# Feed-forward up projection as seven products of quarter matrices, in a two-layer hybrid backbone step

## The chip, the cores and the metric

The kernel runs on one core of a Trainium2 chip. The metric is the device time of one execution in microseconds; lower is better.

## The reference, cut to what matters

One step of a two-layer backbone on 640 tokens (512 latent, 128 context) of 1,024 channels. Each layer has four parallel attention and pooling branches and then a feed-forward part. The change is in the feed-forward part alone:

```
def conv_ffn(h, w_up, conv_w, w_down):
    u = h @ w_up                         # 640 x 1024 by 1024 x 5504
    ...                                  # uc: width-3 convolution of u along the tokens
    a, gt = jnp.split(uc, 2, -1)
    return (jax.nn.silu(gt) * a) @ w_down
```

The hidden width is 2,752, so u has 5,504 columns: the value half a and the gate half gt.

## The kernel before

All products are exact to about float32: every operand x is split into a high part hi, which is x rounded by ScalarE (L144), and a low part lo = x - hi, made by VectorE (L145). A product is then three TensorE passes: hi*hi, hi*lo, lo*hi. `hT` holds the normed input, channels on partitions, as two such parts.

The hidden width is cut into 21 tiles of 128 and a tile 21 of 64 (for which value and gate share one unit). `up_pair` (L1333) makes a tile: for value and for gate it loads 1,024 x 128 weights (L126, on SyncE's queue, into one of two "raw" buffers), splits them (L144, L145) into one of five "w" buffers, and `tposed` (L531) sums 8 channel blocks x 3 passes into a PSUM bank, for 384 and then for 256 tokens (`CH`): 96 matmuls a tile, of 384 or 256 columns. ScalarE copies the banks to `ub` (L1355, L1357, L1358; four buffers). VectorE convolves: a first tap (L1364) and two taps that add (L1366), for each half. Then ScalarE takes a tanh (L1378), VectorE multiplies twice (L1379, L1381), and the result is split into `gT` (L147 on ScalarE, L148 on VectorE).

`ffn_phase` (L1290) goes through the tiles in groups of 4, 4, 4, 4 and 6 (`GRP`). Tiles 0 and 1 are made together (`up_pair(l, ks[:2])`), since their first matmuls can start before all of hT is there. The down projection of a group (`down`, L1397) is written behind the up projection of the next group; 120 matmuls of 512 columns for four tiles. So on TensorE the order of a layer is: 8 tiles up, down, 4 up, down, 4 up, down, 6 up, down, down. In layer 0 up to two pieces of layer 1's modulation (L370) stand behind each tile, each of which loads 1 MB into a "w" buffer.

The instructions of an engine are in an order that the framework's planner works out when the kernel is built: of the instructions that it takes to be ready, the one written first goes first. An engine then runs them strictly in that order, and waits for semaphores in it.

Of the kernel before, what the change touches and what calls it, by code (L numbers as in the profile page):

```python
# [11 lines left out]
F32 = mybir.dt.float32  # L12
F32R = mybir.dt.float32r
# [17 lines left out]
GRP = (4, 4, 4, 4, 6)  # L31
BLOCKS = ((0, 1), (1, 1), (2, 2), (4, 2), (6, 2))
# [64 lines left out]
class Kernel:  # L97
# [22 lines left out]
    # ---------------------------------------------------------------- weights  # L120
    def load(self, src, a, b):
        raw = self.t(self.rawp, [128, 1024], "raw", bufs=2)
# [34 lines left out]
    # ---------------------------------------------------------------- set up  # L157
    def run(self):
        nc, tc = self.nc, self.tc
        from contextlib import ExitStack  # L160
        with ExitStack() as es:
# [5 lines left out]
            self.rawp = es.enter_context(self.pool("raw", bufs=2))  # L167
# [88 lines left out]
    def modulate_block(self, ks, x):  # L256
        """Channel tiles ks of all token tiles: transpose, modulate and split into hT."""
# [18 lines left out]
    def cond(self):  # L276
        nc = self.nc
        raw = self.t(self.rawp, [128, 1024], "raw", bufs=2)[:16]
# [53 lines left out]
    def small(self, l):  # L332
        """The convolution's taps: loads, and a step later their transposes."""
# [47 lines left out]
    def between(self, gen, mod):  # L381
        """gen's pieces with mod's between them."""
# [5 lines left out]
    def before(self, n, gen, other):  # L388
        """n pieces of gen, all of other, and the rest of gen."""
# [4 lines left out]
    def with_steps(self, gen, steps):  # L394
        """gen's pieces with one of steps after each."""
# [5 lines left out]
    def mod_rows(self, l, b, ps, rows):  # L401
        """Modulation rows 2b and 2b+1 of both streams; gates go to DRAM."""
# [10 lines left out]
    def mod_columns(self, l, b, rows):  # L413
        """Shifts and scales become columns."""
# [18 lines left out]
    def mod_gate(self, l, half):  # L433
        nc, i = self.nc, self.i
        L = self.lay[l]
        w = self.t(self.hp, [128, 2, 1280], "yx", bufs=2)
        g, p = w[:16, 0, :128], w[:16, 1, :256]
# [10 lines left out]
    # ------------------------------------------------------------------ norms  # L448
# [9 lines left out]
    def normed(self, y, xt, junk):  # L458
        """y = xt scaled by its root mean square."""
# [6 lines left out]
    def modulate(self, t, y, f, L, half):  # L466
        """Transpose the normed tile y, modulate it and split it into hT; f (which may be y) is scratch."""
# [19 lines left out]
    def prenorm(self, t, x, L, half):  # L487
        """Norm token tile t and modulate the one before."""
# [10 lines left out]
    def gains(self, l, half, pool, tag, width, bufs):  # L499
        """The gate rows times the norm's gain on all partitions, as [stream][half]."""  # L500
# [10 lines left out]
    # ------------------------------------------------------------- projections  # L511
# [28 lines left out]
    def sweep(self, weights_outer, parts, offs):  # L540
        """Token tiles times weights: parts are (lhs_hi, lhs_lo, w_hi, w_lo) by k. Yields a bank per token tile."""
# [27 lines left out]
    # --------------------------------------------------------------- attention  # L569
    def attention_phase(self, l, mod, banks):  # L570
# [6 lines left out]
        with self.pool("att_r", side="right") as ap:  # L577
# [38 lines left out]
            if l == 0:  # L616
                self.mod_gate(l, 0)
# [4 lines left out]
    def weave(self, chain, fill):  # L622
        """Run the chain; wherever it yields a time, let as much of fill pass as takes the tensor engine that time."""
# [10 lines left out]
    def late_y(self, gen):  # L634
        """A branch's output that takes the place of the one that gen still reads: made where it is first written."""
# [1061 lines left out]
```

## Time and profile before

| | us |
|---|---|
| median of three runs | 2185.1 (2182.97 to 2185.57) |
| span of the profiled execution | 2180.6 |
| TensorE busy in it | 2130.0 (98%) |
| VectorE busy | 1216.8 (56%) |
| ScalarE busy | 855.7 (39%) |
| GpSimd busy | 183.3 (8%) |

The span runs from the first to the last instruction; the device time of a run also holds what lies around it. The time of the profiled execution itself is not listed apart; against the three runs its span is 2.4 to 5.0 us shorter. In the profile PE is TensorE's matmuls, PEld its weight loads, DVE VectorE, ACT ScalarE, POOL GpSimd, SP SyncE; L145 is line 145 of the kernel before.

### The profile page before, as it was taken

The numbers are of one execution on the slowest core, as the hardware profiler recorded it, in microseconds if no ns is written. First come the engines' busy times: TensorE is split into PE (matmuls) and PEld (weight loads), VectorE is DVE, ScalarE is ACT, GpSimd is POOL, SyncE is SP. The second block draws the span as 40 slices with busy tenths as digits, with TensorE's granted clock in tenths as the row PEclk, the third lists the DMA queues.
The fourth block names the chain that finished last, engine by engine and source line by source line (L and its number), as shares of the span: only waits on it lengthen the run. The fifth ranks groups of instructions, "written<-read, shape, count | busy, mean of one in ns | idle before, by whom it ended". The sixth has DMA issues, their size and how long they took to land.

```text
span 2180.6 us, 34629 instructions
## 1 busy us (share of the span) xinstructions
PE 2130.0 (98%) x13815; PEld 1928.2 (88%) x13815; DVE 1216.8 (56%) x2207; ACT 855.7 (39%) x1822; POOL 183.3 (8%) x574
## 2 busy tenths in 40 slices
PE   7999999999999999999999999999999999999998
PEld 4779989998889988989878799999998899999996
DVE  3774454653466636456577744556543665556554
ACT  4554344443353333224255543434433533323322
POOL 1102100001021001000021031000000200000001
PEclk9999999999999999999999999999999999999999
DMA  9513221214544444343332132211124322222222
GB/s 303 202 43 101 56 62 46 59 40 156 186 144 150 152 136 156 116 155 89 120 128 81 38 92 64 59 48 52 38 79 154 117 78 78 78 78 78 78 85 94
DMA packets 230476, 221.74 MB, mean 102 GB/s; under 512 B 16084, under 2 KB 196637, under 8 KB 225195
## 3 DMA queue, kind: packets, MB, share of 16 engines
q1 hardware_dynamic: 214000, 191.91, 28.3%
q10 hardware_dynamic: 12026, 21.55, 2.8%
q0 software_dynamic: 4288, 6.07, 1.1%
q8 instruction: 109, 1.79, 0.3%
q14 instruction: 53, 0.43, 0.1%
HBM read 207.94 MB, written 11.56 MB: 101 GB/s over the span
## 4 chain that ended last, share of the span: by engine, by line
PE 89%; DVE 4%; issue 2%; ACT 2%; DMA 1%; POOL 1%; ACTq 0%; DVEq 0%; POOLq 0%
PE mm L536 17%; PE mm L538 16%; PE mm L537 16%; PE mm L548 5%; PE mm L550 5%; PE mm L549 5%; PE tr L155 4%; PE sc L946 3%; PE py L938 2%; PE mm L1227 2%; PE mm L1229 2%; PE mm L1228 2%; PE py L370 1%; PE sc L548 1%; PE sc L549 1%
## 5 line engine op out<-in xcount | busy, mean ns | idle before, releaser
L536 PE MATMUL mm<-hT,w 128*128 128x384 f32 (+1 forms) x2592 | 821.6, 317 | 1.2 <-ACT slab L859 0.9
L538 PE MATMUL mm<-hT,w 128*128 128x384 f32 (+1 forms) x2592 | 801.6, 309 | 1.5 <-DVE w L145 1.5
L537 PE MATMUL mm<-hT,w 128*128 128x384 f32 (+1 forms) x2592 | 800.7, 309 | 0.0
L536 PEld LDWEIGHTS mm<-hT,w 128*128 128x128 f32 x2592 | 491.0, 189 | 33.4 <-issue 17.1
L538 PEld LDWEIGHTS mm<-hT,w 128*128 128x128 f32 x2592 | 491.0, 189 | 3.1 <-DVE w L145 3.1
L537 PEld LDWEIGHTS mm<-hT,w 128*128 128x128 f32 x2592 | 491.4, 190 | 2.0 <-issue 1.4
L145 DVE TENSOR_TENSOR w<-raw,w 128x1024 fp32r<-128x1024 f32 (+2 forms) x263 | 313.4, 1194 | 133.0 <-ACT w L144 131.5
L144 ACT CAST w<-raw 128x1024 fp32r<-128x1024 f32 (+2 forms) x263 | 269.3, 1027 | 205.0 <-PE mm L550 37.3
L1364 DVE TENSOR_SCALAR cv<-ub,taps 128x641 f32<-128x641 f32 x86 | 47.7, 555 | 203.3 <-ACT ub L1358 192.9
L1366 DVE SCALAR_TENSOR_TENSOR cv<-ub,taps,cv 128x641 f32<-128x641 f32 x172 | 152.2, 885 | 5.4
L548 PE MATMUL mm<-w,gT 128*128 128x512 f32 (+1 forms) x352 | 141.4, 402 | 0.0
L549 PE MATMUL mm<-w,gT 128*128 128x512 f32 (+1 forms) x352 | 138.9, 394 | 0.0
L550 PE MATMUL mm<-w,gT 128*128 128x512 f32 (+1 forms) x352 | 138.8, 394 | 0.0
L1209 ACT ACTIVATE th<-mm,cols 128x384 f32<-128x384 f32 (+1 forms) x128 | 67.4, 527 | 148.2 <-PE mm L538 147.9
L1355 ACT COPY ub<-mm 128x384 f32<-128x384 f32 x86 | 41.4, 481 | 164.5 <-PE mm L538 164.4
L1236 DVE SCALAR_TENSOR_TENSOR th<-th,mm 128x384 f32<-128x384 f32 x96 | 45.8, 483 | 100.6 <-PE mm L1229 92.7
L548 PEld LDWEIGHTS mm<-w,gT 128*128 128x128 f32 (+1 forms) x352 | 66.2, 188 | 23.8 <-issue 7.4
L1357 ACT COPY ub<-mm 128x128 f32<-128x128 f32 x86 | 23.0, 267 | 162.4 <-PE mm L538 162.3
L1227 PE MATMUL mm<-yx,w 128*128 128x384 f32 (+1 forms) x256 | 82.8, 323 | 0.0
L1429 DVE TENSOR_TENSOR acc<-acc,mm 128x512 f32<-128x512 f32 x64 | 44.0, 687 | 65.3 <-PE mm L550 64.7
L155 PE MATMUL tr<-cst,P 128*128 128x128 f32 x462 | 67.1, 275 | 13.2 <-DVE P L914 9.2
L550 PEld LDWEIGHTS mm<-w,gT 128*128 128x128 f32 (+1 forms) x352 | 66.0, 188 | 15.7
(305 smaller groups left out, 3152.1 us busy)
## 6 DMA issues: line engine op xcount, KB each, us to landing
w<-in_w_mod_dram SPq DMA_DIRECT2D x46, 1024.0 KB, 4.8
raw<-in_ffn_w_up_dram SPq DMA_DIRECT2D x84, 512.0 KB, 3.9
raw<-in_w_gate_dram SPq DMA_DIRECT2D x64, 512.0 KB, 4.0
raw<-in_ffn_w_down_dram SPq DMA_DIRECT2D x40, 512.0 KB, 3.7
raw<-in_w_in_dram SPq DMA_DIRECT2D x23, 512.0 KB, 4.1
raw<-in_w_out_dram SPq DMA_DIRECT2D x16, 512.0 KB, 6.7
x<-x ACTq DMA_DIRECT2D x14, 512.0 KB, 4.8
raw<-in_w_branch_dram SPq DMA_DIRECT2D x12, 512.0 KB, 3.2
```

The source lines that it names most:

```text
L144: nc.scalar.copy(hi, src)
L145: nc.vector.tensor_tensor(out=lo, in0=src, in1=hi.bitcast(F32), op=ALU.subtract)
L155: self.nc.tensor.transpose(out, in_, ident)
L536: nc.tensor.matmul(ps, lhsT=hi[:, k, :], rhs=self.hT[:, 0, k, o:o + n], start=k == 0, stop=False)
L537: nc.tensor.matmul(ps, lhsT=hi[:, k, :], rhs=self.hT[:, 1, k, o:o + n], start=False, stop=False)
L538: nc.tensor.matmul(ps, lhsT=lo[:, k, :], rhs=self.hT[:, 0, k, o:o + n], start=False, stop=k == KT - 1)
L548: nc.tensor.matmul(ps, lhsT=lh[:, c], rhs=hi, start=q == 0, stop=False)
L549: nc.tensor.matmul(ps, lhsT=lh[:, c], rhs=lo, start=False, stop=False)
L550: nc.tensor.matmul(ps, lhsT=ll[:, c], rhs=hi, start=False, stop=q == n - 1)
L1209: self.anchor = nc.scalar.activation(th[:, :n], pg[:, :n], AF.Tanh, scale=0.5, bias=L['bh'][:, 8 * br + m:8 * br + m + 1]).ins
L1227: nc.tensor.matmul(pb[:, :n], lhsT=hi[:, 0, ms], rhs=y[:, 0, a, cs], start=a == 0, stop=False)
L1366: nc.vector.scalar_tensor_tensor(out=cv, in0=ub[:, j:j + 641], scalar=tp[:, j:j + 1], in1=cv, op0=ALU.mult, op1=ALU.add)
```

## The change

Tiles 1 to 20 of each layer (40 in all) go through a new `up_strassen` in place of `up_pair`; tile 21 moves to the front and is made together with tile 0 by `up_pair` as before (`TILES`). The tile's product, 640 tokens x 1,024 channels by 1,024 channels x 256 columns, is cut into quarters: tokens in two halves of 320, channels in two halves of 512, columns in value and gate. Seven products of quarters (Winograd's form of Strassen's algorithm) replace eight: 7 x 4 channel blocks x 3 passes = 84 matmuls of 320 columns. Sums of token quarters are made once a layer (`combine_tokens`, GpSimd and VectorE, then split), in room of the "yx" tiles, a new "S" tile and hT's own quarter (1,0). Differences of weight quarters are made for each tile: four subtractions of 128 x 512 on GpSimd in the raw buffers, and 3.5 splits of 1,024 columns in four "w" buffers where there were two splits in two. The outputs come from three banks, one of which goes on accumulating after it has been read.

The convolution's first tap goes from VectorE to ScalarE, and the product with the value half from VectorE to GpSimd, for all tiles. There are four raw buffers in place of two; the last residual tile takes a raw buffer, the scratch for GpSimd's DMA descriptors is 4,096 bytes, and `mod_gate` takes the "rows" tile in the feed-forward part in place of a "yx" tile. Lines that only drop comments are left out below.

```
+TILES = (21,) + tuple(range(21))
+HALF_TOK = TOK // 2
+RAWS = 4
+DMA_SCRATCH = 4096
...
@@ ffn_phase
-            ks = list(range(f0, f0 + n))
+            ks = list(TILES[f0:f0 + n])
...
                 gt += self.up_pair(l, ks[:2])
+                self.combine_tokens()
...
-                gt += self.up_pair(l, [k])
+                gt += self.up_strassen(l, k)
...
-                    self.mod_gate(l, 1)
+                    self.mod_gate(l, 1, hold())
...
+    def combine_tokens(self):
+        nc, hT = self.nc, self.hT
+        H = HALF_TOK
+        quarter = lambda i, j: hT[:, :, 4 * j:4 * j + 4, H * i:H * i + H]
...
+        S4 = quarter(1, 0)
...
+        for c in (slice(0, 192), slice(192, H)):
+            for i, j in ((0, 0), (1, 0), (1, 1), (0, 1)):
+                q = quarter(i, j)
+                nc.gpsimd.tensor_tensor(out=f[i, j][:, :, c], in0=q[:, 0, :, c].bitcast(F32),
+                                        in1=q[:, 1, :, c].bitcast(F32), op=ALU.add)
+            a11, a21, a22, a12 = [f[x][:, :, c] for x in ((0, 0), (1, 0), (1, 1), (0, 1))]
+            v = nc.vector
+            v.tensor_tensor(out=a22, in0=a21, in1=a22, op=ALU.add)
+            v.tensor_tensor(out=a21, in0=a11, in1=a21, op=ALU.subtract)
+            v.tensor_tensor(out=a11, in0=a22, in1=a11, op=ALU.subtract)
+            v.tensor_tensor(out=a12, in0=a12, in1=a11, op=ALU.subtract)
+            for S, x in ((S2, a11), (S1, a22), (S3, a21), (S4, a12)):
+                self.split(S[:, 0, :, c], S[:, 1, :, c], x)
+        self.A = {1: quarter(0, 0), 2: quarter(0, 1), 3: S4, 4: quarter(1, 1), 5: S1, 6: S2, 7: S3}
+
+    def up_strassen(self, l, k):
...
+        b11, b21, b12, b22 = ra[:, :512], ra[:, 512:], rg[:, :512], rg[:, 512:]
+        tile = lambda: self.t(self.wp, [128, 2, 1024], "w", F32R)
+        W1 = tile()
+        self.split(W1[:, 0], W1[:, 1], ra)
+        W4 = tile()
+        self.split(W4[:, 0, :512], W4[:, 1, :512], b22)
+        sub = lambda out, x, y: nc.gpsimd.tensor_tensor(out=out, in0=x, in1=y, op=ALU.subtract)
+        sub(b11, b12, b11)
+        sub(b12, b22, b12)
+        sub(b22, b22, b11)
+        W2 = tile()
+        self.split(W2[:, 0], W2[:, 1], rg)
+        sub(b21, b21, b22)
+        W3 = tile()
+        self.split(W3[:, 0], W3[:, 1], ra)
+        B = {1: (W1, 0), 2: (W1, 512), 3: (W4, 0), 4: (W3, 512), 5: (W3, 0), 6: (W2, 512), 7: (W2, 0)}
...
+        Q = self.ps("sc")[:, :H]
+        P = self.ps("mm")[:, :H]
+        product(Q, 1, True)
+        copy(first(ub[0]), Q)
+        product(P, 2, True)
+        add(first(ub[0]), P)
+        product(Q, 6, False)
+        copy(first(ub[1]), Q)
+        R = self.ps("mm")[:, :H]
+        product(R, 5, True)
+        copy(second(ub[1]), R)
+        product(Q, 7, False)
+        add(second(ub[1]), Q)
+        product(R, 3, False)
+        add(first(ub[1]), R)
+        product(Q, 4, False)
+        copy(second(ub[0]), Q)
+        return self.gated(l, [(k, 0, ub[0]), (k, 1, ub[1])])
...
@@ gated (the second half of up_pair before)
-            nc.vector.tensor_scalar(cv, ub[:, 0:641], tp[:, 0:1], None, op0=ALU.mult)
+            nc.scalar.activation(cv, ub[:, 0:641], AF.Copy, scale=tp[:, 0:1])
...
-            nc.vector.tensor_tensor(out=th[:np_], in0=th[:np_], in1=a[:np_], op=ALU.mult)
+            nc.gpsimd.tensor_tensor(out=th[:np_], in0=th[:np_], in1=a[:np_], op=ALU.mult)
```

Here copy is a ScalarE copy from the bank and add a VectorE addition of the bank to what stands in `ub`; "first" is the first 320 tokens, "second" the others, in two pieces of 192 and 128.

## Rows read from the trace of the kernel before

**Rows 1.** The page: the span, and busy time, share and instructions of TensorE.
```profile
span 2180.6 us, 34629 instructions
PE 2130.0 (98%) x13815; PEld 1928.2 (88%) x13815; DVE 1216.8 (56%) x2207; ACT 855.7 (39%) x1822; POOL 183.3 (8%) x574
```

**Rows 2.** Busy time by stretch, layer 1: PE, PEld, DVE, ACT, POOL, clock, DMA.
```profile
1711.60:1715.00 3.40, 3.40 (x15) 3.40 (x14) 3.19 (x7) 3.00 (x7) 0.54 (x1) 0.50 0.57 160
...
1720.76:1826.87 106.11, 106.11 (x733) 106.11 (x732) 68.28 (x86) 40.35 (x80) 3.65 (x42) 1.00 0.27 80
1826.87:1854.71 27.84, 27.84 (x122) 22.56 (x121) 9.56 (x12) 11.08 (x17) 0.55 (x6) 1.00 0.27 76
1854.71:1911.00 56.29, 56.29 (x385) 56.28 (x384) 31.92 (x38) 19.22 (x37) 1.67 (x18) 1.00 0.24 75
2023.02:2100.42 77.40, 77.40 (x529) 77.39 (x528) 47.61 (x57) 26.35 (x51) 2.06 (x21) 1.00 0.30 91
```

**Rows 3.** Timeline of TensorE: start, us, instruction (a matmul's end is modelled).
```profile
418.97 1.05 PE L946 MATMUL sc<-slab,stg 96*128 96x320 f32 x6
...
806.14 1.90 PE L370 MATMUL py<-w,silu_c 128*2 128x512 f32 x16
...
899.85 0.33 PE L536 MATMUL mm<-hT,w 128*128 128x384 f32 x1
...
906.61 0.28 PE L536 MATMUL mm<-hT,w 128*128 128x256 f32 x1
...
912.23 0.29 PE L538 MATMUL mm<-hT,w 128*128 128x256 f32 x1
```

**Rows 4.** Groups by form: busy us, mean ns of one, idle before and releasers.
```profile
L145 DVE TENSOR_TENSOR w<-raw,w 128x1024 fp32r<-128x1024 f32 x245 | 299.8, 1225 | 120.7 <-ACT w L144 119.4
L145 DVE TENSOR_TENSOR hT<-yx,hT 128x512 fp32r<-128x512 f32 x30 | 19.8, 686 | 1.0 <-ACT hT L144 0.6
L1366 DVE SCALAR_TENSOR_TENSOR cv<-ub,taps,cv 128x641 f32<-128x641 f32 x172 | 152.2, 885 | 5.4
L148 DVE SCALAR_TENSOR_TENSOR gT<-tf,gT 128x641 fp32r<-128x641 f32 x42 | 34.7, 826 | 29.3 <-ACT gT L147 29.3
L1429 DVE TENSOR_TENSOR acc<-acc,mm 128x512 f32<-128x512 f32 x64 | 44.0, 687 | 65.3 <-PE mm L550 64.7
L1355 ACT COPY ub<-mm 128x384 f32<-128x384 f32 x86 | 41.4, 481 | 164.5 <-PE mm L538 164.4
L1002 POOL TENSOR_TENSOR T<-T,cst 128x896 f32<-128x896 f32 x8 | 16.9, 2112 | 24.5 <-DMA T<-zd 18.4 <-DVE m L1575 6.1
L536 PEld LDWEIGHTS mm<-hT,w 128*128 128x128 f32 x2592 | 491.0, 189 | 33.4 <-issue 17.1 <-ACT w L144 6.9 <-ACT ub L1358 3.5
```

**Rows 5.** Timeline of VectorE and GpSimd where both are at work.
```profile
636.64 2.35 DVE L145 TENSOR_TENSOR w<-raw,w 128x1024 fp32r<-128x1024 f32 x2
637.46 1.58 POOL L453 TENSOR_SCALAR ms<-ss 128x1 f32<-128x1 f32 x1 [4.09 <-ACT yx L462]
...
1343.60 2.11 POOL L1002 TENSOR_TENSOR T<-T,cst 128x896 f32<-128x896 f32 x1 [3.13 <-DMA T<-zd]
1344.48 2.31 DVE L145 TENSOR_TENSOR w<-raw,w 128x1024 fp32r<-128x1024 f32 x1
...
1017.62 0.59 POOL L445 TENSOR_TENSOR yx<-yx 16x128 f32<-16x128 f32 x1
1017.93 0.97 DVE L1366 SCALAR_TENSOR_TENSOR cv<-ub,taps,cv 128x641 f32<-128x641 f32 x1
...
1740.77 1.68 DVE L1366 SCALAR_TENSOR_TENSOR cv<-ub,taps,cv 128x641 f32<-128x641 f32 x2
1741.79 0.10 POOL L1346 MEMSET ub<- 128x1 f32 x1 [3.34 <-DVE cv L1366]
```

**Rows 6.** Timeline: token tile 3's last split, both layers; layer 0's first down matmul.
```profile
648.05 0.68 DVE L145 TENSOR_TENSOR hT<-yx,hT 128x512 fp32r<-128x512 f32 x1
...
764.07 0.47 PE L548 MATMUL mm<-w,gT 128*128 128x512 f32 x1
...
1718.56 0.69 DVE L145 TENSOR_TENSOR hT<-yx,hT 128x512 fp32r<-128x512 f32 x1
```

More of the change, by code (lines that the diff above doesn't have):

```diff
@@ L431, in mod_columns, with mod_gate @@
                 nc.vector.tensor_tensor(out=o, in0=o, in1=col(L['gpre'][half]), op=ALU.mult)
[L433 removed]
+    def mod_gate(self, l, half, w):
         nc, i = self.nc, self.i
         L = self.lay[l]
[L436 to L437 removed]
+        g, p = w[:16, :128], w[:16, 128:384]
         nc.gpsimd.dma_start(out=g, in_=L['mod'][half].rearrange("s k p -> (s k) p"))
@@ L1327, in ffn_phase @@
             for half in range(2):
-                self.mod_gate(nxt, half)
+                self.mod_gate(nxt, half, hold())
         self.down(l, *pend)
@@ new lines, in up_strassen, with product, copy, add @@
+    def up_strassen(self, l, k):
+        nc, i = self.nc, self.i
+        w = i['ffn_w_up'][l].rearrange("(k p) n -> p k n", p=128)
+        ra, rg = [self.load(w[:, :, s * D_FF + 128 * k:s * D_FF + 128 * k + 128], KT, 128)[0] for s in range(2)]
+        b11, b21, b12, b22 = ra[:, :512], ra[:, 512:], rg[:, :512], rg[:, 512:]
[14 more added lines that the diff above has]
+        B = {1: (W1, 0), 2: (W1, 512), 3: (W4, 0), 4: (W3, 512), 5: (W3, 0), 6: (W2, 512), 7: (W2, 0)}
+        H = HALF_TOK
+        def product(ps, m, start):
+            W, o = B[m]
+            A = self.A[m]
+            for q in range(4):
+                hi, lo = W[:, 0, o + 128 * q:o + 128 * q + 128], W[:, 1, o + 128 * q:o + 128 * q + 128]
+                nc.tensor.matmul(ps, lhsT=hi, rhs=A[:, 0, q, :], start=start and q == 0, stop=False,
+                                 skip_group_check=True)
+                nc.tensor.matmul(ps, lhsT=hi, rhs=A[:, 1, q, :], start=False, stop=False, skip_group_check=True)
+                nc.tensor.matmul(ps, lhsT=lo, rhs=A[:, 0, q, :], start=False, stop=q == 3, skip_group_check=True)
+        ub = [self.t(self.fp, [128, 643], "ub", bufs=4) for _ in range(2)]
+        for u in ub:
+            nc.gpsimd.memset(u[:, 0:1], 0.0)
+            nc.gpsimd.memset(u[:, 513:514], 0.0)
+            nc.gpsimd.memset(u[:, 642:643], 0.0)
+        first = lambda u: [(u[:, 1:1 + H], slice(0, H))]
+        second = lambda u: [(u[:, 1 + H:513], slice(0, 512 - H)), (u[:, 514:642], slice(512 - H, H))]
+        def copy(places, ps):
+            for u, c in places:
+                nc.scalar.copy(u, ps[:, c])
+        def add(places, ps):
+            for u, c in places:
+                nc.vector.tensor_tensor(out=u, in0=u, in1=ps[:, c], op=ALU.add)
+        Q = self.ps("sc")[:, :H]
[16 more added lines that the diff above has]
+        return self.gated(l, [(k, 0, ub[0]), (k, 1, ub[1])])
@@ L1368, in up_pair @@
             conv[k, s] = cv
-        for k in ks:
+        for k in dict.fromkeys(k for k, _, _ in work):
             gt = self.t(self.gp, [128, 2, 642], "gT", F32R, bufs=8)
@@ L1395, in unit_pair, with down @@
         return v[:, 0], v[:, 1]
-    def down(self, l, g, f0, gts):
+    def down(self, l, g, gts):
         nc, i = self.nc, self.i
@@ L1413, in down @@
                 rows = i['ffn_w_down'][l]
-                if n1 == 128:
+                if n1 == 128 and pr[-1][0] == k + 1:
                     u = self.unit(rows[128 * k:128 * k + 256, hs].rearrange("(a p) n -> p a n", p=128), 2, 512)
                 else:
-                    u = self.unit_ragged(rows, k, hs)
+                    u = self.unit_ragged(rows, [x[0] for x in pr], hs)
                 for b, (kk, gt, np_) in enumerate(pr):
@@ L1450, in residual @@
         if t == 2:
-            x = self.t(self.fp, [128, D], "x", bufs=1)
+            x = self.t(self.rawp, [128, 1024], "raw", bufs=RAWS)
         else:
```

37 lines of the change are left out of this document (23 added, 14 removed).

## The prediction

> **What bounds the kernel now.** I read the page first, for who is busy: TensorE works through 98% of the span [rows 1]. Then the stretches of layer 1's feed-forward part, where TensorE has no gap at all, neither in four up tiles (56.3 us) nor in the down products of four tiles (27.8 us), while VectorE is busy for 31.9 of 56.3 us and GpSimd for 1.7 [rows 2]. So a matmul saved there is time saved, as long as the other engines keep up. Then TensorE's timeline, for the price of a matmul: from 899.85 to 906.61 stand 39 of 384 columns, 173 ns each; from 906.61 to 912.23 47 of 256 columns, 120 ns each; six of 320 columns, in another stage, take 1.05 us, of which the last one's modelled end is 0.31, so about 148 ns each [rows 3]. Last I looked for places where VectorE and GpSimd work at once, since the change gives GpSimd work [rows 5].
>
> **TensorE.** A tile is now 48 x 0.173 + 48 x 0.120 = 14.1 us; four of them are the 56.3 us of rows 2. After, 84 matmuls of 320 columns at 0.147 (the mean of the two prices) are 12.3 us. 40 tiles x 1.76 = **-70.4 us**. Tile 21 only moves. In layer 0 two pieces of modulation behind a tile add 1.9 us [rows 3], before as after.
>
> **VectorE and GpSimd.** What they do to each other: at 1344.48 VectorE starts a split of 1,024 columns beside a GpSimd addition that ends at 1345.71. The split takes 2.31 us, where the mean is 1.225; it ends 1.08 us after GpSimd [rows 4, 5]. At 1017.93 a convolution tap stretches to 0.97 us and ends 0.69 us after GpSimd's L445, where the mean is 0.885. The other way round, a GpSimd operation on 128 x 1 waits through two splits for 1.58 us (637.46). So a VectorE operation with two inputs in SBUF and a GpSimd operation that reads SBUF do not run together; they share something exclusive. A memset of GpSimd passes beside a tap in 0.10 us, and operations that read PSUM are not counted among those that share.
>
> Work of this shared kind for one new tile, by whole durations [rows 4]:
> - weight splits on VectorE: 3 x 1.225 + 0.686 = 4.36; four subtractions of 512 on GpSimd, at 2.112 us / 896 = 2.36 ns an element, 4 x 1.21 = 4.83. Together 9.2.
> - gating: four taps x 0.885, the product behind the tanh and the split of gT, both as L148, 0.83 each: 5.2 on VectorE; the product of 641 on GpSimd 1.5. Together 6.7.
>
> That is 15.9 us a tile against TensorE's 12.3. It is the upper end. If only the stretches that really excluded each other count (1.08 and 0.69 of VectorE's durations, GpSimd whole), it is 7.9 + 6.3 = 14.3. Two splits in a row take 2.35 and two taps 1.68 [rows 5], so a follower costs 1.13 and 0.80: with these, 8.7 + 6.3 = **15.0**, which I take. VectorE's additions from banks (shorter than the 0.69 us of a 512-column one) read PSUM and fit beside GpSimd.
>
> A stage of down products has 27.8 us of TensorE and little VectorE work, so a backlog can be worked off there; what matters is each run of up tiles: 6 new tiles, 4, 4, 6 in each layer. The weights of a run's first tile come ready during the stage before; tile 1 leaves 12.3 - 9.2 = 3.1 us of the shared time free, and the last weights of a tile are not needed before its fourth product, 3 x 1.76 = 5.3 us in. So a run has 8.4 us of grace; from its third tile on it falls behind by 15.0 - 12.3 = 2.7 us a tile in layer 1, and by 0.7 behind modulation in layer 0.
> - Runs of four: 2 x 2.7 is less than 8.4, no stall: 49.3 instead of 56.3, four times, -28.
> - Last run, layer 1: 4 x 2.7 - 8.4 = 2.4 late, 73.9 + 2.4 instead of 77.4 [rows 2]: -1.1. Layer 0, where modulation covers two tiles: -3.5.
> - **First runs.** They have no grace, because the sums of token quarters come in there. GpSimd adds 4 x 768 and 4 x 512 elements, 12.1 us; VectorE has 8 operations of 768 and 8 of 512 columns, 13.1 us, all of the shared kind: 25.2. They cannot start before token tile 3 is split (1719.25 and 648.73, rows 6). From there on the shared work is 1.4 (last splits of hT) + 25.2 + 11.6 (gating of tiles 21 and 0) + 6 x 9.2 + 4 x 6.7 (the gating of the last two tiles can wait for the down stage) - 1.9 (splits made earlier) = 118.2, at 15.0 / 15.9 of it 111.5; four products, 7.0 us, follow the last weights. Layer 1 ends its run at 1719.25 + 118.5 = 1837.8, before at 1826.9 [rows 2]: +10.9. Layer 0 ends at 767.2, before at 764.07 [rows 6]: +3.2. Without the shared work both would be 17.6 us earlier than before.
>
> Sum: -28 - 1.1 - 3.5 + 10.9 + 3.2 = -18.5. So about 52 of the 70.4 us are given back as waits for weights. At 15.9 the same steps give +17.6, +9.9, -28, +2.5, -1.5: +0.5. At 14.3 they give +5.7, -2.0, -28, -3.5, -3.5: -31.3.
>
> **The rest.** Banks: a bank that goes on accumulating must be read within one product, 1.76 us; a copy takes under 0.48 us [rows 4], but may stand behind a weight split's cast on ScalarE. Now such a wait is 3.5 us in the whole kernel [rows 4]. I take +2, with 0 and +40 (1 us a tile) as ends. ScalarE, 19.2 us in 56.3 now [rows 2], gets one and a half casts and two taps more a tile and stays under TensorE. `mod_gate` puts GpSimd's subtractions behind its DMA waits, three times in layer 0; I take 0, at most a few us, since layer 0 has the modulation as cover. Weight DMAs keep number and size, at 0.24 to 0.30 of the engines [rows 2]: 0. More raw buffers elsewhere and the smaller descriptor scratch: 0, some 5 us either way. A long stall can halve TensorE's clock for a while, as in the 3.4 us from 1711.6 (0.50, rows 2), behind a stretch in which it mostly waited for hT: at most some 2 us each.
>
> Total -16.5. The profiled span is 4.5 us under the median, and I leave what lies around it as it is: 2185.1 - 16.5 = **2169**.
>
> **Rivals.**
> 1. *The two engines hardly hold each other up.* VectorE alone has about 11 us a tile, under 12.3; then only the token sums show, some 5 us a layer: -70.4 + 10 + 2, **2127**. For it: one tap alone shows the hold, by 0.08 us, and the memset passes. Against it: 2.31 and 0.97 end where a full exclusion puts them [rows 5]. The note under "VectorE Performance Modes" of the Trainium skill's page "Advanced Engine Details and Errata" names only VectorE's two-port modes as blocking GpSimd, which gives this case; the trace disagrees with it on the split of two tensors.
> 2. *No change.* Every operation excludes the other engine for all of its duration, 15.9 a tile: +0.5 + 2, **2188**. Against it: 1.08 and 0.69 are less than the whole durations. The Trainium skill's page "SBUF — State Buffer", "SBUF: two separate sides", says that the shared ports are an exclusive lock held for the whole instruction, for VectorE operations with two SBUF inputs against GpSimd operations that read; the trace agrees on who excludes whom, less on the length.
> 3. *Slower: GpSimd is starved and the weights come late everywhere.* The subtractions feed two of the four weight splits. A GpSimd operation waits while VectorE runs one operation behind another (1.58 us, of which 1.4 waiting), and ScalarE, which rounds the difference next, stands in its order with bank copies queued behind it, which TensorE needs. With 1.5 us of this a tile in which neither engine gets on, 17.4 a tile: first runs +28.7 and +21.0, runs of four -24.4 together, last runs +8.5 and +4.5, banks +2: +40, **2225**. It decides from about 15.8 us a tile on. For it: the order of each engine is fixed ahead, and the planner may not know of the exclusion. Against it: VectorE often waits for ScalarE (29.3 us before the gT splits alone, rows 4), and there GpSimd gets its turn.
>
> **How the numbers follow.** My forecast (14.3 to just under 15.8 a tile) 0.50, rival 1 0.15, rival 2 0.13, rival 3 0.22. About 4.4 us, 0.2%, is what a measurement of this kernel can tell from no change. Faster: 0.50 + 0.15 = 0.65. Same: 0.13. Slower: 0.22. The forecast's own range is 2150 to 2182. The range for 8 in 10 takes in rival 2, most of rival 1 and the nearer part of rival 3: 2130 to 2208.
>
> **What would show it.** The 84 matmuls should stand 0.147 us apart. In the runs of four TensorE should be almost without gaps, about 49 us; in the first run of each layer its idle time should be some 20 to 28 us, released by the weight splits of VectorE or ScalarE, and VectorE's splits and taps should show stretched durations (over 2 us and near 1.5 us) beside GpSimd's. If these durations stay at 1.22 and 0.89, rival 1 holds. If the runs of four stall too, with weight loads waiting in every tile, rival 3 does. I am wrong if banks, not weights, release TensorE, or if the time goes to another stage.

## The result and the profile after

| | us |
|---|---|
| before, median of four runs on the same chip | 2185.3 (2183.0 to 2187.7) |
| after, median of four runs | 2303.3 (2303.1 to 2305.5) |
| ratio | 1.0544, 95% interval 1.0529 to 1.0559 |

The change costs 118 us; predicted were 16 less. First the page of the changed kernel, against [rows 1]:

```profile
span 2301.3 us, 34235 instructions
PE 2121.1 (92%) x13335; PEld 1886.6 (82%) x13335; DVE 1377.7 (60%) x2349; ACT 987.4 (43%) x2004; POOL 527.7 (23%) x794
```

480 matmuls are gone (40 tiles x 12), but TensorE is busy for only 9 us less, since for some of the time it runs at half speed; and its idle time has gone from 51 to 180 us. GpSimd has gone from 183 to 528 us. Where the time went, by stretches of TensorE's timeline in layer 1 (from a first to a last matmul):

| us | before | predicted | after |
|---|---|---|---|
| the pair's first matmul to the first down matmul | 118.3 | 129.2 | 155.3 |
| first run of four | 56.3 | 49.3 | 59.5 |
| second run of four | 56.3 | 49.3 | 59.4 |
| last run | 77.4 | 76.3 | 92.0 |

Layer 0 loses as much: its first down matmul stands at 793.0 instead of 764.1 (predicted 767.2), its runs of four take 74.3 and 63.4 instead of 64.3 and 61.8, its last run 102.2 instead of 81.0; the prediction's steps give 57.3, 54.8 and 77.5 for the three. (The last run has six whole tiles now and had five and a half, the first half a tile more; the prediction counted it so.)

Busy time by stretch in layer 1, which answers to [rows 2] (PE, PEld, DVE, ACT, POOL, granted clock, DMA share, GB/s); the first run's Strassen tiles, a run of four, the last run, and one tile of the last run, from one wait to the next:

```profile
1797.36:1924.52 127.16, 83.94 (x507) 81.22 (x506) 93.90 (x105) 54.93 (x96) 64.61 (x71) 0.83 0.19 53
1954.54:2014.00 59.46, 53.22 (x338) 52.40 (x338) 41.85 (x51) 29.70 (x51) 24.10 (x33) 0.94 0.28 81
2129.95:2221.93 91.98, 78.89 (x506) 76.74 (x505) 66.95 (x79) 44.14 (x77) 40.90 (x49) 0.96 0.28 81
2175.37:2192.11 16.74, 12.85 (x86) 12.32 (x85) 12.20 (x15) 7.78 (x15) 8.55 (x11) 1.00 0.23 63
```

Read the last line first. A tile takes 16.74 us, TensorE is busy for 12.85 of them; VectorE's 12.20 and GpSimd's 8.55 add up to 20.75, more than the tile. Laid on one time axis, one of the two or both are at work for 15.74 of 16.74 us, for 5.0 of them both by the record. VectorE's additions from banks take no longer beside GpSimd (0.48 us for 320 columns with it and without); in most of the other overlaps one is held by the other. The groups by form show it in the durations, against [rows 4]; the last two lines have shortest, median and longest of the taps and of three of four differences, in ns:

```profile
L149 DVE TENSOR_TENSOR w<-raw,w 128x1024 fp32r<-128x1024 f32 x285 | 356.3, 1256 | 172.2 <-ACT w L148 167.4 <-PE mm L1397 0.9
L1472 DVE SCALAR_TENSOR_TENSOR cv<-ub,taps,cv 128x641 f32<-128x641 f32 x172 | 196.5, 1199 | 3.9 <-ACT cv L1470 3.6
L1377 POOL TENSOR_TENSOR raw<-raw,raw 128x512 f32<-128x512 f32 x120 | 182.0, 1517 | 310.5 <-DVE w L149 298.5 <-DMA raw<-in_ffn_w_up_dram 6.7 <-ACT ub L1409 1.2
L1487 POOL TENSOR_TENSOR tf<-tf,cv 128x641 f32<-128x641 f32 x42 | 74.1, 1764 | 85.0 <-DVE tf L1485 85.0
L1353 POOL TENSOR_TENSOR gT<-hT 128x768 f32<-128x768 f32 x8 | 16.4, 2079 | 0.0
...
L1472 DVE SCALAR_TENSOR_TENSOR cv<-ub,taps,cv x172: 871/882/1940, 662.0 to 2227.0; 128x641 f32<-128x641 f32 x172
L1377 POOL TENSOR_TENSOR raw<-raw,raw x120: 1263/1306/1876, 645.7 to 2203.6; 128x512 f32<-128x512 f32 x120
```

In the mean a tap takes 1.20 us instead of 0.885, a difference on GpSimd 1.52 where 1.21 was worked out.

The timeline shows the two places where TensorE stands. The first six lines are layer 1's token sums, the rest is one wait of the last run (start, us, instruction, in brackets the idle time before it and what released it):

```profile
1786.21 0.69 DVE L149 TENSOR_TENSOR hT<-yx,hT 128x512 fp32r<-128x512 f32 x1 [0.20 <-ACT hT L148]
...
1811.64 1.53 POOL L1487 TENSOR_TENSOR tf<-tf,cv 128x641 f32<-128x641 f32 x1
1813.13 15.45 POOL L1353 TENSOR_TENSOR gT<-hT 128x768 f32<-128x768 f32 x8
...
1819.10 2.54 DVE L1357 TENSOR_TENSOR gT<-gT,gT 128x768 f32<-128x768 f32 x1 [3.45 <-POOL gT L1353]
1821.68 1.90 DVE L1358 TENSOR_TENSOR gT<-gT,gT 128x768 f32<-128x768 f32 x1
...
1833.30 0.64 PE L1394 MATMUL mm<-yx,w 128*128 128x320 f32 x1 [30.09 <-ACT yx L148]
...
2168.32 3.13 POOL L1377 TENSOR_TENSOR raw<-raw,raw 128x512 f32<-128x512 f32 x2 [0.87 <-DVE w L149]
2171.41 1.58 POOL L1487 TENSOR_TENSOR tf<-tf,cv 128x641 f32<-128x641 f32 x1
2178.71 1.88 POOL L1377 TENSOR_TENSOR raw<-raw,raw 128x512 f32<-128x512 f32 x1 [5.72 <-DVE w L149]
...
2173.80 0.83 DVE L152 SCALAR_TENSOR_TENSOR gT<-tf,gT 128x641 fp32r<-128x641 f32 x1 [4.43 <-ACT gT L151]
...
2178.55 5.36 DVE L1472 SCALAR_TENSOR_TENSOR cv<-ub,taps,cv 128x641 f32<-128x641 f32 x4
...
2173.02 0.74 ACT L151 ACTIVATE gT<-tf 128x641 fp32r<-128x641 f32 x1 [4.70 <-POOL tf L1487]
2173.67 1.99 ACT L148 CAST w<-raw 128x1024 fp32r<-128x1024 f32 x2
2175.57 0.46 ACT L1409 COPY ub<-sc 128x192 f32<-128x192 f32 x2
2175.93 1.05 ACT L148 CAST w<-raw 128x1024 fp32r<-128x1024 f32 x1
2176.88 1.55 ACT L1470 ACTIVATE cv<-ub,taps 128x641 f32<-128x641 f32 x2
2178.33 0.41 ACT L1409 COPY ub<-sc 128x320 f32<-128x320 f32 x1
...
2178.79 0.41 PE L1394 MATMUL sc<-yx,w 128*128 128x320 f32 x1 [3.12 <-ACT ub L1409]
```

The sums: hT's last split in this stretch ends at 1786.9, the first sum starts at 1813.13, behind a gate product; TensorE, which had done three products that need no sums (36 matmuls), stood for 30.1 us. In the last run: GpSimd's gate product ends at 2173.0, only then ScalarE rounds gT, and behind that, in its fixed order, come casts, copies and taps, and at 2178.33 the copy of the bank that TensorE wants for its third product. In layer 1 there is such a wait, of 1.5 to 3.1 us, in nearly every tile from the third of a run on.

The clock has a part too. Its mean is 0.970 (before 0.998): mostly behind waits TensorE is granted 0.5 (1.2 of 2.4 GHz) for a while, in 21 stretches of 139.5 us in all. One of 34.1 us is for the most part its idle time at layer 1's sums. In the others a matmul of 320 columns starts 0.267 us after the one before instead of 0.147. 316 matmuls start in these stretches; at 0.12 us more for 320 columns, and others in proportion, some 41 us is my estimate of what the clock costs. In the run of four above, with two stretches of 3.4 us at 0.50, TensorE is busy for 53.2 us, and 49.3 of them would do at the full clock.

### The profile page after: what moved, and what is told of

It reads as the page before. It is cut to its first block, busy times and chain, and to the rows that moved or that the text cites. A ratio compares the mean times of both kernels' runs of the same rounds, so it can differ in the third digit from the quotient of the medians.

```text
span 2301.3 us, 34235 instructions
## 1 busy us (share of the span) xinstructions
PE 2121.1 (92%) x13335; PEld 1886.6 (82%) x13335; DVE 1377.7 (60%) x2349; ACT 987.4 (43%) x2004; POOL 527.7 (23%) x794
## 5 line engine op out<-in xcount | busy, mean ns | idle before, releaser
L149 DVE TENSOR_TENSOR w<-raw,w 128x1024 fp32r<-128x1024 f32 (+2 forms) x343 | 410.9, 1204 | 182.0 <-ACT w L148 176.5
L148 ACT CAST w<-raw 128x1024 fp32r<-128x1024 f32 (+2 forms) x343 | 333.7, 979 | 264.0 <-PE sc L553 71.3
L539 PE MATMUL mm<-hT,w 128*128 128x256 f32 (+1 forms) x1312 | 425.1, 324 | 0.6 <-ACT hT L148 0.4
L541 PE MATMUL mm<-hT,w 128*128 128x256 f32 (+1 forms) x1312 | 406.5, 310 | 1.5 <-DVE w L149 1.5
L540 PE MATMUL mm<-hT,w 128*128 128x256 f32 (+1 forms) x1312 | 405.6, 309 | 0.0
L539 PEld LDWEIGHTS mm<-hT,w 128*128 128x128 f32 x1312 | 248.2, 189 | 22.2 <-issue 17.1
L1377 POOL TENSOR_TENSOR raw<-raw,raw 128x512 f32<-128x512 f32 x120 | 182.0, 1517 | 310.5 <-DVE w L149 298.5
L541 PEld LDWEIGHTS mm<-hT,w 128*128 128x128 f32 x1312 | 248.2, 189 | 3.1 <-DVE w L149 3.1
L540 PEld LDWEIGHTS mm<-hT,w 128*128 128x128 f32 x1312 | 248.6, 189 | 1.8 <-issue 1.4
L1472 DVE SCALAR_TENSOR_TENSOR cv<-ub,taps,cv 128x641 f32<-128x641 f32 x172 | 196.5, 1199 | 3.9 <-ACT cv L1470 3.6
L1394 PE MATMUL sc<-yx,w 128*128 128x320 f32 x160 | 60.5, 378 | 55.8 <-ACT ub L1409 55.8
L1394 PE MATMUL sc<-hT,w 128*128 128x320 f32 x320 | 102.6, 321 | 9.3 <-DVE ub L1413 7.0
L1394 PE MATMUL mm<-hT,w 128*128 128x320 f32 x320 | 100.9, 315 | 4.5 <-ACT ub L1409 4.4
L1397 PE MATMUL sc<-hT,w 128*128 128x320 f32 x320 | 100.1, 313 | 1.0 <-DVE w L149 0.8
L1487 POOL TENSOR_TENSOR tf<-tf,cv 128x641 f32<-128x641 f32 (+1 forms) x44 | 79.5, 1807 | 91.1 <-DVE tf L1485 91.1
L1396 PE MATMUL sc<-hT,w 128*128 128x320 f32 x320 | 100.3, 313 | 0.0
L1397 PE MATMUL mm<-hT,w 128*128 128x320 f32 x320 | 99.5, 311 | 0.0
```

The source lines that it names most:

```text
L148: nc.scalar.copy(hi, src)
L149: nc.vector.tensor_tensor(out=lo, in0=src, in1=hi.bitcast(F32), op=ALU.subtract)
L539: nc.tensor.matmul(ps, lhsT=hi[:, k, :], rhs=self.hT[:, 0, k, o:o + n], start=k == 0, stop=False)
L540: nc.tensor.matmul(ps, lhsT=hi[:, k, :], rhs=self.hT[:, 1, k, o:o + n], start=False, stop=False)
L541: nc.tensor.matmul(ps, lhsT=lo[:, k, :], rhs=self.hT[:, 0, k, o:o + n], start=False, stop=k == KT - 1)
L1377: sub = lambda out, x, y: nc.gpsimd.tensor_tensor(out=out, in0=x, in1=y, op=ALU.subtract)
```

## The experiments

Theory **T**: VectorE and GpSimd exclude each other, and the sum of their work paces a Strassen tile. Theory **S**: the token sums come late by GpSimd's order. Rivals: **G**, ScalarE's in-order queue, held behind a late GpSimd product; **B**, the banks that must be read in time; **E**, the other edits; **D**, the chain from difference to weights, not the load; **W**, the amount of work in the first run, whatever its order. Times of a single run stand beside 2183 to 2185 us of the kernel before on the same chip.

**The other edits alone.**
```
-                self.combine_tokens()
-                gt += self.up_strassen(l, k)
+                gt += self.up_pair(l, [k])
```


> All tiles go through the ordinary product of 96 matmuls; the token sums and weight differences are not needed and not made. The other edits stay: first tap on ScalarE, gate product on GpSimd, four raw buffers, tile 21 first. Theory T (in a Strassen tile VectorE and GpSimd, which exclude each other, are busy one or the other for 15.7 of 16.7 us, and that sets the pace): an ordinary tile has only some 9 us of such work against 14.1 us of TensorE, so no new waits: 2178 to 2195 us, as before. Rival E (the moved tap and gate product themselves cost, by copies of banks standing behind them on ScalarE): over 2220, with waits of TensorE for the copies in most tiles.


2184.7 us: E falls. Its rows are what ordinary tiles take in this order of tiles (first run with the rest of the pair, a run of four, a last run of six):
```profile
1722.56:1821.25 98.69, 98.69 (x683) 98.69 (x682) 53.80 (x64) 48.49 (x93) 14.70 (x46) 1.00 0.25 71
1851.16:1907.71 56.55, 56.55 (x386) 56.55 (x386) 25.75 (x28) 24.02 (x44) 5.64 (x21) 1.00 0.24 75
2019.57:2104.17 84.60, 84.60 (x578) 84.60 (x577) 40.54 (x44) 35.85 (x66) 9.11 (x29) 1.00 0.28 82
```

**No weight differences.**
```
-        sub(b11, b12, b11)
...
-        sub(b21, b21, b22)
```


> Left out: the four weight differences of GpSimd in each Strassen tile (the weights go into the same splits undiffered, so the output is not the reference's). Everything else stays, all matmuls too. Theory T: the shared time of VectorE and GpSimd falls from 15.7 to some 10 us a tile, under TensorE's 12.3; runs of four in layer 1 go from 59.4 to 49.3-51 us, the last run from 92 to 74-77; the first run keeps its wait of some 30 us for the token sums. In all 2185 to 2220. Rival B (the banks that go on accumulating must be read in time by a ScalarE that works in order, whatever the load): runs of four stay above 57, time above 2270.


2201.6 us; runs of four 51.5, last run 78.2, the wait at the sums still there (27 us). With four GpSimd operations fewer per tile, same matmuls, same banks and same copies, three quarters of what the later runs had over TensorE's own time (49.3 and 74.0) is gone: B falls.

**Differences and gate product on VectorE.**
```
-        sub = lambda out, x, y: nc.gpsimd.tensor_tensor(out=out, in0=x, in1=y, op=ALU.subtract)
+        sub = lambda out, x, y: nc.vector.tensor_tensor(out=out, in0=x, in1=y, op=ALU.subtract)
...
-            nc.gpsimd.tensor_tensor(out=th[:np_], in0=th[:np_], in1=a[:np_], op=ALU.mult)
+            nc.vector.tensor_tensor(out=th[:np_], in0=th[:np_], in1=a[:np_], op=ALU.mult)
```


> The four weight differences and the gate product go from GpSimd to VectorE (a difference of 512 columns should take 0.69 us there instead of 1.54, the product 0.83 instead of 1.76). Theory T: the union of both engines falls from 15.7 to about 14.6 us a tile, VectorE nearly alone: still over 12.3, so waits stay but are smaller: runs of four 53 to 57, last run of layer 1 some 83, in all 2250 to 2280. Rival G (the loss is GpSimd's place in the fixed order, gT's rounding standing on ScalarE behind a late GpSimd product): waits vanish with GpSimd, runs of four 49 to 51, in all 2190 to 2225. Rival B: no change, 2295 to 2310.


2220.5 us, 83 less than after, by giving the busier engine more to do. The total lies in G's range, the runs of four (52.9) lie between the two. But the two tiles from 2097.05 to 2125.32 (second row) show what paces them:
```profile
2056.62:2139.95 83.33, 79.07 (x506) 76.75 (x505) 74.13 (x104) 45.20 (x77) 1.26 (x24) 0.96 0.30 89
2097.05:2125.32 28.27, 26.55 (x172) 24.96 (x171) 27.50 (x39) 16.59 (x30) 0.63 (x12) 1.00 0.27 75
```
VectorE is busy for 27.50 of 28.27 us, 13.8 a tile, and the waits of this run are for weights (the longest 1.0 and 2.0 us, released by ScalarE's and VectorE's halves of a split). T has the mechanism, and its figure was too high: VectorE needs 13.8 us a tile, not 14.6. Part of the 83 us is won at the sums, where TensorE waits 18.4 us instead of 30.1, with no gate product ahead of them on GpSimd.

**A late gate product.** The gate product and the split of gT were to be issued behind the next tile's second copy.
```
+        last = copy(first(ub[1]), Q)
+        with self.tc.issue_after(last):
+            self.finish()
```


> Same instructions, other order: the gate product on GpSimd and the split of gT of a tile are issued behind the next tile's copy of the bank that stalls now, so that this copy can no longer stand on ScalarE behind the rounding of gT. Theory T: the shared work per tile is the same, so the pace stays 16 to 17 us a tile, the waits only change their place or releaser; 2290 to 2315. Rival G: the wait of 3.4 us a tile at the third product goes, with the halved clock behind it: runs of four 50 to 53, in all 2225 to 2260.


2300.1 us, which tells nothing: in the runs of layer 1 ScalarE's order came out as it was, since gT already stood behind that copy. So the next was made.

**A later split of gT,** two tiles on, behind the very copy that TensorE waits for:
```
+        last = copy(first(ub[0]), Q)
+        with self.tc.issue_after(last):
+            self.finish(2)
```


> The same instructions, but ScalarE's rounding of gT of a Strassen tile is issued behind the copy of the bank of the first product two tiles later, which is the copy that TensorE waits for now; so that copy can no longer stand behind a rounding that waits for GpSimd. Theory T (VectorE and GpSimd together are busy 15.7 of 16.7 us a tile): at best the 0.8 us go in which both wait for ScalarE; runs of four 57 to 60 us, in all 2285 to 2306, with new releasers of the waits. Rival G (ScalarE's in-order queue behind GpSimd is what costs): the 3.4 us per tile and the halved clock behind them go: runs of four 50 to 53, in all 2225 to 2260.


2282.9 us; runs of four 54.7 and 56.1, last run 86.0. G has a part: 20 us. What remains fits T; a tile of the last run:
```profile
2161.45:2177.01 15.56, 12.88 (x84) 12.32 (x84) 12.22 (x15) 7.88 (x16) 8.45 (x12) 1.00 0.24 72
```
From 2150 to 2185 VectorE or GpSimd is at work in 34.84 of 35.0 us, with no gap over 0.15. The pace is 15.56, and the 1.0 us in which neither worked is gone. Such a full axis alone does not tell exclusion from a chain: in each tile VectorE stands 3.3 us until ScalarE has rounded one of GpSimd's differences, and GpSimd 3.8 until VectorE has made a weight split. But the amount fits exclusion. VectorE's 13.8 us of the run before, less its differences (2.9), gate product (0.9) and additions from banks (1.5), are 8.5; GpSimd's four differences and its product, at their shortest (1.26 and 1.53), are 6.6. So 15.1 of the 15.56 is work that could not overlap, by this estimate.

**Sums ahead of the gating.**
```
-                gt += self.up_pair(l, ks[:2])
-                self.combine_tokens()
+                gt += self.up_pair(l, ks[:2], self.combine_tokens)
...
+        if between is not None:
+            between()
         return [x for k in ks for x in self.gated(l, [(k, s, ub) for kk, s, u, ub in work if kk == k])]
```


> The sums of token quarters are written ahead of the gating of tiles 21 and 0 (after their banks are copied) and not behind it; the same instructions otherwise. Theory S (they came late, at 1813 us, only because GpSimd's fixed order has two gate products and three differences ahead of the first sum, and TensorE then stood for 30.4 us in layer 1): GpSimd's first sum starts as soon as hT is there, the wait falls from 30.4 to 5-12 us, the first run of layer 1 from 127.2 to 98-110 us; in all 2250 to 2275. Rival W (it is the amount of shared work in front of the first run, 118 us by the prediction, and the order of it does not matter): the wait is only split up among the tiles of that run, its length stays above 120 us; in all 2292 to 2306.


2279.2 us. GpSimd's sums in its timeline, two of the three lines; they start as hT's tokens come:
```profile
1775.37 1.83 POOL L1352 TENSOR_TENSOR gT<-hT 128x768 f32<-128x768 f32 x1 [2.64 <-DVE hT L149]
1785.51 5.60 POOL L1352 TENSOR_TENSOR gT<-hT 128x768 f32<-128x768 f32 x3
```
No wait for the sums is left in layer 1, and its first run takes 102.6 us instead of 127.2: S, against W. The total is 4 us above the range, because layer 0's first run won only 4 us.

**Idle differences.** The differences left out, the gate product on VectorE, and in layer 1 GpSimd subtracts scratch.
```
+        if l == 1:
+            d = self.t(self.fp, [128, 512], "rows", bufs=1)
+            nc.gpsimd.memset(d, 0.0)
+            for _ in range(4):
+                nc.gpsimd.tensor_tensor(out=d, in0=d, in1=d, op=ALU.subtract)
```


> As without the weight differences (left out, so the output is not the reference's; that kernel took 2201.6), with the gate product on VectorE, and in layer 1 alone GpSimd makes four subtractions of 128x512 per Strassen tile on scratch that nobody reads. Layer 0 has none. Theory T (exclusion: GpSimd's work costs VectorE its own time even if nobody waits for the result): VectorE's operations in layer 1 are stretched as before (taps over 1.1 us in the mean, differences 1.4 to 1.7 us), union of both some 14 to 15 us a tile, runs of four 53 to 58 and the last run 80 to 90; in all 2210 to 2235. Rival D (what costs is that the weights wait for the differences, a chain, not the load): runs of four 50 to 52 and the last run 75 to 79 in layer 1, in all 2194 to 2204.


2227.1 us, but not as meant: nothing held the 80 subtractions to their tiles, all ran in the first run, which took 156.7 us. What it shows is the rest, without GpSimd: in layer 1's later runs TensorE has no gap at all.
```profile
1917.40:1966.90 49.50, 49.50 (x337) 49.41 (x337) 38.89 (x53) 30.71 (x51) 0.99 (x18) 1.00 0.34 97
2072.00:2146.00 74.00, 74.00 (x503) 73.59 (x502) 61.32 (x84) 45.89 (x77) 1.32 (x24) 1.00 0.35 100
```

**Differences that nobody reads,** but of the tile's own weights:
```
+            for x, y in ((b12, b11), (b22, b12), (b22, b11), (b21, b22)):
+                nc.gpsimd.tensor_tensor(out=d, in0=x, in1=y, op=ALU.subtract)
```


> As the run with idle subtractions, whose 80 subtractions ran ahead into the first run of layer 1, but now each reads its own tile's raw weights, as the real differences do, so it can't run ahead; it writes scratch that nobody reads. Layer 1 only; the weights go into the splits undiffered, the gate product is on VectorE. Theory T (exclusion, by load): GpSimd's four subtractions a tile (1.2 to 1.9 us each) take the shared time from VectorE's 10.2 us a tile; union 15 to 16 us, VectorE's taps over 1.1 us in the mean, runs of four 53 to 60 and the last run 80 to 92 us in layer 1. Rival D (what costs is that the weight splits wait for the differences): runs of four 49.3 to 51.5 and the last run 74 to 78, as without the subtractions (49.5 and 74.0).


2206.8 us. Runs of four 51.1 (D's figure; T said 53 to 60), last run 81.2 (nearly T's), and 33.3 and 31.7 us for the down stages behind the runs of four instead of 28.1. A stretch of the last run, and the taps in this kernel and in the one before (idle differences), both behind the first run:
```profile
2062.00:2093.00 31.00, 29.41 (x198) 28.78 (x197) 30.24 (x34) 17.52 (x32) 15.96 (x21) 1.00 0.26 72
...
L1471 DVE SCALAR_TENSOR_TENSOR cv<-ub,taps,cv 128x641 f32<-128x641 f32 x52 | 50.8, 1040 | 0.0
...
L1472 DVE SCALAR_TENSOR_TENSOR cv<-ub,taps,cv 128x641 f32<-128x641 f32 x56 | 45.8, 881 | 0.0
```
Here the two engines' 46.2 us of records fill 31.0 us without a gap; a tap takes 1.04 us in the mean from the second run on, and 0.88 without GpSimd's work. So the load alone costs VectorE its time, and TensorE waits for VectorE's additions from banks. From the first down matmul to the end of layer 1's last run this kernel takes 278 us, the one without GpSimd's work 259, the changed one 297: about half of the 38 us is load that nobody waits for. Where nobody waits, GpSimd's work slides into the down stages. The other half must lie in what this kernel lacks: weights that wait for the differences, and the gate product on GpSimd. No run separates the two.

**Towards a faster kernel.** First with differences and gate product on VectorE, the sums early and tile 1 ordinary behind them:
```
+                gt += self.up_strassen(l, k) if k > 1 else self.up_pair(l, [k])
```


> A kernel that should be faster by theory: differences and gate product on VectorE (2220.5 us alone), sums of token quarters (on GpSimd) written ahead of the gating, and tile 1 of each layer an ordinary tile, as cover for the sums (it costs 1.8 us a layer). Theories T and S: runs of four 51 to 53 in layer 1, the wait for sums under 5 us instead of 18.9 with the halved clock behind it; in all 2160 to 2190. If the shared work of the first run is what counts (rival W): 2205 to 2222.


2198.3 us, 8 above the range. Tile 1 reads hT when the sums have already overwritten a quarter of it, so this computes something else, and tile 1 waits for the sums (3.8 us in layer 1) rather than cover them.

Then with that quarter overwritten behind tile 1 (`last`), and tiles 17 and 19 ordinary:
```
+                gt += self.up_pair(l, ks[2:3])
+                self.last()
...
+                gt += self.up_strassen(l, k) if k not in (17, 19) else self.up_pair(l, [k])
```


> Differences, gate product and token sums all on VectorE; the sums are written ahead of the gating of tiles 21 and 0, tile 1 of each layer is ordinary and stands as cover behind them (hT's own quarter is overwritten only behind it), and tiles 17 and 19 of each layer are ordinary too, since VectorE needs 13.8 us for a Strassen tile and about 8 for an ordinary one, so that four and two together stay under TensorE's time. Theories T and S: wait for the sums under 4 us a layer, runs of four 51 to 53, last run of layer 1 77.4 to 79.5 (before 84.5); in all 2150 to 2178. Rival W (the first run's amount of shared work counts, order does not): first run as long as in the kernel with differences on VectorE, in all 2185 to 2210.

> As the one with all on VectorE, but the eight first additions of the token sums are on GpSimd (1.8 to 2.0 us each for 768 columns, where VectorE takes 0.97 for such an operation alone). Theory T: more shared time in the first run, by some 5 to 8 us, of which the cover tile hides most: 2152 to 2188, no faster than the other.


2181.8 and 2189.7 us, both 2 to 4 above their ranges, and times only: tiles 17 and 19 read the overwritten quarter. Layer 1's last run takes 77.4 us, as worked out, and the sums cost 8 us more on GpSimd than on VectorE. All of a layer's ordinary tiles must stand ahead of its first Strassen tile. So, with combine_tokens in three parts on VectorE:

```
+COVER, LAYERS = 3, (1,)
...
+                if l in LAYERS and k > COVER:
+                    gt += self.up_strassen(l, k)
+                else:
+                    gt += self.up_pair(l, [k])
+                    if l in LAYERS and k in (1, COVER):
+                        next(self.sums)
```


> A kernel that should beat both by theories T and S. Layer 0 is ordinary throughout; in layer 1 tiles 21, 0, 1, 2 and 3 are ordinary and stand as cover, the token sums are made on VectorE behind tiles 0 and 1 and the quarter of hT itself is overwritten behind tile 3, before the first Strassen tile (4), so that no ordinary tile reads the changed hT. Differences and gate product on VectorE. Expected in layer 1: no wait for sums, first run 93 to 98 us (98.7 with ordinary tiles alone), runs of four 52 to 53 (56.5), last run 83 to 84 (84.6); in all 2168 to 2180. If the first run stalls as before (rival W): 2180 to 2195.


**2172.7 us** (median of five, 2171.9 to 2177.5) against 2184.2 (nine runs): ratio 0.9951, interval 0.9937 to 0.9964. It beats both kernels. Its profiled execution is the slowest of the five; layer 1's first run, a run of four and the last run:
```profile
1721.40:1822.70 101.30, 97.25 (x649) 95.21 (x648) 89.64 (x123) 58.03 (x106) 2.04 (x39) 0.98 0.20 60
1852.40:1905.10 52.70, 51.04 (x339) 49.68 (x339) 46.72 (x66) 30.36 (x51) 0.94 (x18) 1.00 0.28 85
2013.70:2096.80 83.10, 78.90 (x505) 76.53 (x504) 73.90 (x104) 45.15 (x77) 1.25 (x24) 0.96 0.30 89
```
The first run of four gives 3.8 us against the ordinary tiles' 56.55, the second 2.6 (53.7 against 56.3), the last run 1.5; the first run, with VectorE busy for 89.6 of 101.3 us, costs 2.6 where its three Strassen tiles save TensorE 5.3.

The same with everything on GpSimd that the change puts there:


> As the one for layer 1 alone, but sums, differences and gate product on GpSimd as in the changed kernel. Theory T: same order, same cover, only the engine differs: runs of four 58 to 60, last run 90 to 93, first run 96 to 106; in all 2192 to 2206. If the engine hardly matters once the sums have cover (rival S alone): 2168 to 2185.


2223.2 us: 50.5 more for the engine alone, with the sums under cover, and nearly all of it in layer 1 (in layer 0, where only the gate products move, it is 0.8). The long runs are back (a run of four, the last run):
```profile
1876.50:1934.30 57.80, 51.76 (x338) 50.94 (x338) 41.60 (x50) 29.81 (x51) 24.12 (x33) 0.97 0.26 82
2050.40:2142.10 91.70, 78.64 (x505) 76.49 (x504) 66.73 (x79) 44.13 (x77) 40.84 (x49) 0.96 0.27 81
```
The total is above the range because the first run takes 123.8 us, not 96 to 106: work on GpSimd holds VectorE up beside the ordinary tiles too (a tap takes 1.04 us in that run, 0.88 in the faster kernel's).

And the faster kernel with layer 0 as well:


> As the one for layer 1 alone, but in both layers. Theory M (in layer 0 the pieces of modulation between the tiles, each with 1 MB of weights to load and a w buffer, set the pace, so fewer matmuls give nothing there): layer 0 as long as with ordinary tiles within 5 us either way, 2168 to 2186. Rival: layer 0 gains what layer 1 gains, 2158 to 2167.


2179.7 us: layer 0 loses 7 us, so this kernel does not have layer 1's gain there. 6 of the 7 are lost in its first run, in which the sums stand: VectorE is busy for 85.8 of 99.6 us (666.0 to 765.6), and TensorE waits 3.4 us for weights of the modulation. Its first run of four loses 3.7, its second wins 2.9. The first row is that run of four; the other two are layer 0's first and last of these runs in the kernel with idle differences, which has no differences at all in layer 0:
```profile
795.40:863.40 68.00, 62.58 (x402) 52.87 (x401) 47.48 (x66) 31.44 (x54) 0.98 (x18) 0.95 0.51 181
...
802.20:862.14 59.94, 59.94 (x401) 50.58 (x400) 39.56 (x54) 30.70 (x54) 0.99 (x18) 1.00 0.61 201
...
974.29:1054.41 80.12, 79.70 (x534) 74.88 (x532) 64.97 (x89) 47.59 (x80) 11.81 (x40) 1.00 0.40 126
```
In the first row VectorE is busy for 47.5 of 68.0 us and TensorE waits for weights all the same (the longest wait 2.1 us, for ScalarE's half of a split). Ordinary tiles take 64.3 there. A Strassen tile holds four of the five w buffers, and the modulation takes one for each of its pieces. But this alone is not the cause: with the same buffers and the same modulation, only without the differences, the runs take 59.9, 56.3 and 80.1 us, against 64.4, 61.8 and 88.1 with ordinary tiles, and TensorE has next to no gap. So M does not hold as it was put; Strassen tiles do gain in layer 0, until the differences come. How these cost so much where VectorE is not full stays open. More buffers were not tried.

## Why the prediction was wrong

It said 2169, with 2130 to 2208 and 0.65 for faster. Rival 3, at 0.22, had the sign, the mechanism and the pace (17.4 us a tile; 16.7 measured), and was 78 us too low in its total. Of the 134 us between forecast and result, some 52 lie in the two first runs, 36 in layer 1's later runs and 50 in layer 0's, by the differences from the predicted lengths. Point by point:

- **TensorE, -70.4.** Right. A product of 12 matmuls takes 1.76 us, and six tiles without GpSimd's work take 74.0.
- **Who excludes whom.** Right, and for more of the duration than I took. The Trainium skill's page "SBUF — State Buffer", "SBUF: two separate sides", has an exclusive lock for the whole instruction. The trace comes near it: the longest tap takes 1.94 us, 1.06 more than the median, where a difference takes 1.26 at its shortest. The note in "VectorE Performance Modes" of the Trainium skill's page "Advanced Engine Details and Errata", on which rival 1 rested, names only two-port modes; these operations are held up too: a tap goes from 0.885 to 1.20 us in the mean.
- **15.0 us of shared work a tile.** Too small: 15.56 where nothing else holds the engines, 15.74 and 1.0 of common idling in the changed kernel. I took the row of followers over the whole durations, and 1.21 us for a difference that takes at least 1.26. VectorE's additions from banks do fit beside GpSimd, as I said. (The lower end, 7.9 + 6.3 = 14.3, has its parts wrong: 1.08 and 0.69 give 8.7 + 5.6, the same sum.)
- **"A run has 8.4 us of grace", the step that failed most.** I let a late weight reach TensorE only at the fourth product. The lateness came a product earlier and by another way: ScalarE stands waiting for GpSimd's results, and in its order the copy of the bank comes behind the casts and taps that it does then. So the deficit shows from the third tile on, with nothing to spare: two waits of 3.1 and 2.8 in a run of four. Instead of 7 us less, each takes 3 more in layer 1; the last run takes 92.0 instead of 76.3. Together 36 us of layer 1's error. Even at 15.56 a tile the runs of four took 54.7 and 56.1, where the 8.4 would have left 49.3.
- **First runs, +10.9 and +3.2.** +37 and +29 measured. I spread the sums over the run as shared work that starts when hT is there. They started 26 us later, because the framework puts GpSimd's gate product and differences ahead, and then went through two engines one after the other, with TensorE idle. Putting them first won 24 us.
- **Banks, +2.** I named it a sign of being wrong if banks release TensorE, and in layer 1's later runs a bank's copy ends all of its waits over 0.3 us (25.3 us; 56.9 in 23 waits at the first bank in the whole kernel). But the bank is only where it shows: with the same banks and no differences the waits go. (Two of the three banks go on accumulating after they have been read, Q and R, not one.)
- **The clock.** "At most some 2 us each" is right for a stretch of 3.4 us: a product at half clock takes 3.2 instead of 1.76. I did not count how many stalls there would be: 21 stretches, some 41 us by the estimate above.
- **Layer 0.** I counted its modulation as cover: no stall in the runs of four, 3.5 us won in the last. They take 74.3, 63.4 and 102.2 instead of 57.3, 54.8 and 77.5, together 50 us. Modulation does not prevent the gain by itself (without differences TensorE has next to no gap there), but it covered nothing of what the differences cost; by which path is not shown.

## What to carry to other kernels

Before work goes to GpSimd as the idle engine, add its operations to VectorE's wherever both read SBUF, and compare the sum with the bound engine's time; here VectorE alone did the same work in 13.8 us a tile that the two did in 15.6 to 16.7. A reserve worked out for one wait is worth only as much as the shortest path by which the same lateness reaches the bound engine, and in-order queues with bank copies make that path short. A preparation that is made once must be placed ahead in each engine's order, with work behind it that doesn't need it.

## What was unexpected of the hardware

- Four differences and one product cost less on the engine that was at 60% than on the one at 23%: 0.72 us on VectorE against 1.52 on GpSimd for 128x512, and the kernel became 83 us faster. The Trainium skill's page "Perfetto Trace Analysis", "Optimizing Scalar/DVE Operations", warns that moving operations between these two might not help; here it did harm.
- Short waits cost TensorE's clock again and again. In the kernel before, the feed-forward part has no wait to speak of, and one stretch at 0.50 [rows 2]; with a wait of some 3 us in nearly every tile the mean of a run of four falls to 0.94, of a first run with a long wait to 0.83.
